# A seven-product group in which block 12 is only ever added by transfers

## The chip, the cores and the metric

The kernel runs on one core of a Trainium2 chip. The metric is the device time of one execution in microseconds (us): 1966.47 is the median of three runs (1966.36 to 1967.82).

## The reference

A decoder layer on 256 tokens (two blocks of 128) with 2048 channels: a SwiGLU FFN of 5632 columns, a mixer of two attention branches, and a second FFN, each with a residual and a layer norm. Nearly all the work is matrix products in float32:

```python
def _swiglu(x, w_gate, w_up, w_down):
    return (jax.nn.silu(x @ w_gate) * (x @ w_up)) @ w_down
...
    c_q, c_kv, k_r, dq, dk, dv, gate_mla, gate_diff = _split_columns(h @ w_in)
...
    y = jax.nn.sigmoid(gate_mla) * (o_mla @ w_br_mla) + jax.nn.sigmoid(gate_diff) * (o_diff @ w_br_diff)
    return y @ w_out
```

## The kernel before, in words

**Split products.** A float32 product is made of three faster ones. Each weight block (128 x 1024, two contraction tiles of 128 by 512 columns) is loaded, cast by ScalarE to a high part (line 154), and VectorE subtracts that from the block to get the low part (line 155). TensorE then does high x high, high x low and low x high (lines 208 to 210). The two parts of a block lie in one of six pairs of a ring (`wring`); a split can start when the products of the unit six before it have read that pair.

**Units and their order.** A unit is a load, a split (`prep`) and its products (`now`). The program issues a unit's load three units ahead of its split, and the split up to four units ahead of its products. Nothing else orders the work: the engines run what was issued, in the order in which a scheduler has put each engine's line, and wait for each other by semaphores. SyncE issues the plain loads, GpSimd (POOL) the transfers that add to what is there, the rows of the hidden layer that go to memory and come back (`hT`), and the mixer's turned rows (`turn`, `turned`) and gates.

**Groups of seven products.** The class `Hybrid` takes two column chunks of 512 (`w0`, `w1`) as a group. Over the first eight of sixteen contraction tiles it multiplies 2 x 2 blocks by seven products instead of eight. The blocks are named by contraction half and chunk: 11 (w0, first), 12 (w1, first), 21 (w0, second), 22 (w1, second). A product has two units (s = 0, 1); in a *wide* group it has a third, half as large (`eraw`), from one contraction tile pair more. The rest of the contraction is *plain* units, p for w0 and q for w1, twelve matmuls each against six in a product's unit. A string gives the order, as "15pp6p72q4q3q" for a wide group.

The weights of the products are sums, made in place on the raw blocks:

- 1 reads 11; 5 reads 11 + 12; 6 reads 11 + 12 + 22; 4 reads 11 + 12 + 22 + 21: VectorE adds to 11 ahead of each of the three (line 430).
- 7 reads 12 + 22: in the FFNs a transfer adds 22 from memory to 12 (line 432); in the mixer (`small`) VectorE does.
- 2 reads 21, and 3 reads 22.

The products' results go to banks X, Z, Y and W, and some of these sums are copied out midway (lines 387, 388), since the next product goes on adding in the same bank.

Each FFN's up projection has ten groups, of which the eight in the middle are wide. The mixer has six narrow ones: three for gates, then dq, dk and dv; in these last three, block 21 uses the buffer of 12 (`share`). A group runs to its end before the next begins. The down projections have a class of their own and aren't part of the change.

## Time and profile before

| | |
|---|---|
| runs, median of 3 | 1966.47 us |
| the profiled execution: its own time, first to last instruction | 1963.9 us, mean granted clock 0.998 |
| TensorE busy | 1952.0 us, 99% |
| VectorE busy | 1779.9 us, 91% |
| ScalarE busy | 1251.5 us, 64% |
| POOL busy | 312.1 us, 16% |
| transfers | 488.86 MB, of which 86.09 MB by GpSimd's queue (q0) |
| adding transfers (line 432) | 40 of 512 KB, 16 of 256 KB |

In the rows below, L154 is line 154 of the kernel; a group of instructions shows its busy time, the mean of one in ns, then the engine's idle time before it and what ended that. PE is TensorE, DVE VectorE, ACT ScalarE, POOL GpSimd, SP SyncE. The view by stretches gives, for each stretch, every engine's busy time and number of instructions, then the granted clock, the mean busy share of the sixteen DMA engines and GB/s. Matmuls are pipelined, so the time from start to start says what one costs.

The first FFN's groups lie at about 40 to 425 us, its down projection follows to about 700, the mixer's groups are at about 720 to 965, and the second FFN's groups at about 1300 to 1690.

### The profile page before, as it was taken

To read this page: it belongs to the slowest core of one execution; us is meant where nothing else is said; L and a number is where in the kernel's file an instruction comes from. 1 tells how busy PE (TensorE), PEld (TensorE's weight loads), DVE (VectorE), ACT (ScalarE), POOL (GpSimd) and SP (SyncE) were. 2 spreads that over 40 slices of the span, in tenths; PEclk is the share of its full clock that TensorE was granted. 3 is DMA by queue.
4 is the path that set the end of the run, shared out by engine and by line. 5 is a ranking of instruction groups with operands and counts; after the bars stand their busy time and mean duration, and the time that the engine had idled before them with its cause. 6 is when DMAs were issued, how large, how long until landed. Compare 5 with 4: busy or idle time off the path is not lost.

```text
span 1963.9 us, 25802 instructions
## 1 busy us (share of the span) xinstructions
PE 1952.0 (99%) x8763; PEld 1617.7 (82%) x8763; DVE 1779.9 (91%) x2189; ACT 1251.5 (64%) x1640; POOL 312.1 (16%) x536
## 2 busy tenths in 40 slices
PE   9999999999999999999999999999999999999998
PEld 7888888888888898888788888888888888888886
DVE  7999999999998879988987777789999999999997
ACT  6666766676655566666667655556676666665662
POOL 0112111122100010102241530001211112210000
PEclk9999999999999999999999999999999999999999
DMA  8978888878776667767685798587888878787773
GB/s 314 289 225 262 270 260 249 257 233 300 272 235 222 210 216 258 239 223 252 211 254 195 237 305 271 201 264 254 252 269 263 250 240 277 241 318 236 277 232 124
DMA packets 150228, 488.86 MB, mean 249 GB/s; under 512 B 21792, under 2 KB 22096, under 8 KB 150096
## 3 DMA queue, kind: packets, MB, share of 16 engines
q1 hardware_dynamic: 119232, 401.00, 59.7%
q0 software_dynamic: 30720, 86.09, 16.8%
q8 instruction: 68, 1.11, 0.2%
q14 instruction: 64, 0.52, 0.1%
q10 hardware_dynamic: 144, 0.13, 0.0%
HBM read 456.73 MB, written 30.41 MB: 248 GB/s over the span
## 4 chain that ended last, share of the span: by engine, by line
PE 95%; DVE 2%; DMA 1%; issue 1%; ACT 0%; POOL 0%; SPq 0%; DVEq 0%; ACTq 0%; POOLq 0%
PE mm L208 30%; PE mm L210 30%; PE mm L209 30%; DVE wring L155 1%; PE tr L208 1%; PE tr L210 1%; PE tr L209 1%; PE tr L673 0%; DMA turned<-turn 0%; ACT wring L154 0%; DMA sraw<-in_wdk_dram 0%; DVE sraw L430 0%; PE tr L1376 0%; PE tr L1304 0%; PE tr L1378 0%
## 5 line engine op out<-in xcount | busy, mean ns | idle before, releaser
L154 ACT CAST wring<-raw 128x1024 fp32r<-128x1024 f32 (+2 forms) x468 | 482.7, 1035 | 323.5 <-PE mm L210 237.6
L155 DVE TENSOR_TENSOR wring<-raw,wring 128x1024 fp32r<-128x1024 f32 (+2 forms) x468 | 557.0, 1198 | 95.6 <-ACT wring L154 93.5
L154 ACT CAST wring<-sraw 128x1024 fp32r<-128x1024 f32 x436 | 453.1, 1052 | 201.7 <-DVE sraw L430 83.6
L155 DVE TENSOR_TENSOR wring<-sraw,wring 128x1024 fp32r<-128x1024 f32 x436 | 520.3, 1218 | 20.6 <-ACT wring L154 17.8
L208 PE MATMUL mm<-wring,h 128*128 128x512 f32 (+2 forms) x1248 | 480.9, 385 | 0.1
L210 PE MATMUL mm<-wring,h 128*128 128x512 f32 (+2 forms) x1248 | 480.3, 385 | 0.0
L209 PE MATMUL mm<-wring,h 128*128 128x512 f32 (+2 forms) x1248 | 479.9, 385 | 0.0
L208 PE MATMUL mm<-wring,xs 128*128 128x512 f32 x776 | 302.2, 389 | 0.5 <-ACT snap L387 0.5
L209 PE MATMUL mm<-wring,xs 128*128 128x512 f32 x776 | 302.1, 389 | 0.0
L210 PE MATMUL mm<-wring,xs 128*128 128x512 f32 x776 | 301.9, 389 | 0.0
L210 PEld LDWEIGHTS mm<-wring,h 128*128 128x128 f32 x1248 | 234.4, 188 | 47.0 <-DVE h L155 0.7
L208 PEld LDWEIGHTS mm<-wring,h 128*128 128x128 f32 x1248 | 234.4, 188 | 46.7 <-ACT h L154 0.6
L209 PEld LDWEIGHTS mm<-wring,h 128*128 128x128 f32 x1248 | 234.4, 188 | 46.1
L430 DVE TENSOR_TENSOR sraw<-sraw,sraw 128x1024 f32<-128x1024 f32 x168 | 199.1, 1217 | 2.0 <-DMA sraw<-in_wdk_dram 1.6
L208 PEld LDWEIGHTS mm<-wring,xs 128*128 128x128 f32 x776 | 145.6, 188 | 31.0 <-ACT snap L387 0.9
L209 PEld LDWEIGHTS mm<-wring,xs 128*128 128x128 f32 x776 | 145.7, 188 | 30.5 <-DVE wring L155 0.3
L210 PEld LDWEIGHTS mm<-wring,xs 128*128 128x128 f32 x776 | 145.7, 188 | 30.2
L719 POOL DMA_DIRECT2D hT<-blocks x176 | 96.8, 563 | 368.3 <-DVE blocks L717 367.2
L209 PE MATMUL mm<-wring,x 128*128 128x512 f32 x336 | 130.9, 390 | 0.2 <-DVE wring L155 0.2
L208 PE MATMUL mm<-wring,x 128*128 128x512 f32 x336 | 130.1, 390 | 0.8 <-ACT wring L154 0.8
L210 PE MATMUL mm<-wring,x 128*128 128x512 f32 x336 | 130.7, 389 | 0.0
L432 POOL DMA_DIRECT2D sraw<-in_gu_dram x40 | 35.6, 892 | 371.4 <-DVE sraw L430 334.5
(328 smaller groups left out, 2292.4 us busy)
## 6 DMA issues: line engine op xcount, KB each, us to landing
sraw<-in_gu_dram SPq DMA_DIRECT2D x160, 512.0 KB, 5.2
raw<-in_gu_dram SPq DMA_DIRECT2D x158, 512.0 KB, 5.0
raw<-in_dn_dram SPq DMA_DIRECT2D x140, 512.0 KB, 4.7
sraw<-in_gu_dram POOLq DMA_DIRECT2D x40, 512.0 KB, 7.5
sraw<-in_dn_dram SPq DMA_DIRECT2D x36, 512.0 KB, 5.4
eraw<-in_gu_dram SPq DMA_DIRECT2D x64, 256.0 KB, 5.8
raw<-in_w_out_dram SPq DMA_DIRECT2D x32, 512.0 KB, 4.3
hraw<-hT POOLq DMA_DIRECT2D x56, 256.0 KB, 5.9
```

The lines of the kernel that those rows point to most:

```text
L154: cast[0] = S.copy(hi, src)
L155: lows[0] = V.tensor_tensor(out=lo, in0=src, in1=hi.bitcast(F32), op=ALU.subtract)
L208: PE.matmul(o, xh, wh, start=first, stop=False, skip_group_check=again)
L209: PE.matmul(o, xh, wl, start=False, stop=False, skip_group_check=again)
L210: PE.matmul(o, xl, wh, start=False, stop=last, skip_group_check=again)
L430: last = V.tensor_tensor(out=R[src][i], in0=R[src][i], in1=R[add[1]][i], op=ALU.add)
L432: nc.gpsimd.dma_start(R["12"][s], source("22", s), accum_op=ALU.add)
L719: nc.gpsimd.dma_start(to.rearrange("(g r) (i f) -> i r g f", g=4, i=4)[i], t[32 * i:32 * (i + 1), :].rearrange("r (g f) -> r g f", g=4))
```

## The change

Block 12 has no buffer any more. After 1 is split, a transfer adds 12 to 11 for product 5; after 6 is split, another adds 12 to 22 for product 7. VectorE adds 22 to 11 for 6, and for 4 adds 11 to 21 as soon as 2 has been split (before, 21 to 11 ahead of 4). The mixer's groups do the same as the FFN's, so `share` goes. Product 3 stands ahead of 6. The first product of a group is issued ahead of the last product (4) and plain units of the group before it (the n in the string); for this the groups are handed over as a list (`run`). Bank Z comes from the three banks of the transposes.

```diff
-            plan = {1: ("11", "11", None, "X"), 5: ("12", "11", ("11", "12"), "Z"), 6: ("22", "11", ("11", "22"), "X"),
-                    7: (None, "12", ("12", "22"), "X"), 2: ("21", "21", None, "Y"), 4: (None, "11", ("11", "21"), "W"),
-                    3: (None, "22", None, "Z")}
+            plan = {1: ("11", "11", None, "X"), 5: (None, "11", None, "Z"), 3: ("22", "22", None, "Z"),
+                    6: (None, "11", "22", "X"), 7: (None, "22", None, "X"), 2: ("21", "21", None, "Y"),
+                    4: (None, "21", None, "W")}
+            added = {1: "11", 6: "22"}
...
-                    banks[n] = mm_bank()
+                    banks[n] = tr_bank() if n == "Z" else mm_bank()
...
-                    if not small and p == 6:
-                        nc.gpsimd.dma_start(R["12"][s], source("22", s), accum_op=ALU.add)
                     pair = [v[:, :tiles * 512] for v in next_pair()]
                     with tc.issue_after(last.ins) if last is not None and not small else nullcontext():
                         split_in_line(not small, *pair, t)
+                    if p in added:
+                        nc.gpsimd.dma_start(R[added[p]][s], source("12", s), accum_op=ALU.add)
+                    elif p == 2:
+                        with nullcontext() if small else behind_split(1):
+                            V.tensor_tensor(out=t, in0=t, in1=R["11"][s], op=ALU.add)
...
-            if self.shared:
-                order = "15pp6p7p3q2q4qq" if seeded else "1p5p6p7p3q2q4qq"
-            elif wide:
-                order = "15pp6p72q4q3q"
-            elif seeded:
-                order = "15pp6p7p2q4q3qq"
-            else:
-                order = "1p5p6p7p2q4q3qq"
+            order = "1p5p36p27qn4qq" if wide else "1p5p36pp27qn4qqq" if self.begun else "1ppp5p3627qn4qqq"
...
+        def run(self, groups):
+
+            parts = [self.group(*g[:-1]) for g in groups]
+            for i, (order, emit) in enumerate(parts):
+                if groups[i][-1] is not None:
+                    groups[i][-1]()
+                for c in order if i == 0 else order[1:]:
+                    if c != "n":
+                        emit(c)
+                    elif i + 1 < len(parts):
+                        parts[i + 1][1]("1")
```

In the second FFN the three blocks that are fetched ahead are now 11, 22 and 21 (before: 11, 12 and 22).

What this does to the lines of the engines is shown at three places.

VectorE, a wide group of the first FFN, from the additions for 6 to the end of 2. Before, `sraw_463`, `464` and `eraw_471` are block 11, `465`, `466` 12, `467`, `468` 22 and `469`, `470`, `eraw_472` 21 (`eraw` holds two blocks each):

```order
L430 TENSOR_TENSOR sraw_463<-sraw_463,sraw_467 128x1024
L430 TENSOR_TENSOR sraw_464<-sraw_464,sraw_468 128x1024
L430 TENSOR_TENSOR eraw_471<-eraw_471,eraw_472 128x512
L155 TENSOR_TENSOR wring_121<-sraw_463,wring_120 128x1024
L155 TENSOR_TENSOR wring_119<-sraw_464,wring_118 128x1024
L155 TENSOR_TENSOR wring_117<-eraw_471,wring_116 128x512
L155 TENSOR_TENSOR wring_115<-raw_1453,wring_114 128x1024
L155 TENSOR_TENSOR wring_105<-sraw_465,wring_104 128x1024
L155 TENSOR_TENSOR wring_103<-sraw_466,wring_102 128x1024
```

After, `sraw_463`, `464` are 11, `465`, `466` 22 and `467`, `468` 21 (`eraw_469` holds 11 and 22, `eraw_470` 21):

```order
L155 TENSOR_TENSOR wring_117<-eraw_469,wring_116 128x512
L438 TENSOR_TENSOR sraw_463<-sraw_463,sraw_465 128x1024
L438 TENSOR_TENSOR sraw_464<-sraw_464,sraw_466 128x1024
L438 TENSOR_TENSOR eraw_469<-eraw_469 128x512
L155 TENSOR_TENSOR wring_115<-sraw_463,wring_114 128x1024
L155 TENSOR_TENSOR wring_105<-sraw_464,wring_104 128x1024
L155 TENSOR_TENSOR wring_103<-eraw_469,wring_102 128x512
L155 TENSOR_TENSOR wring_121<-raw_1469,wring_120 128x1024
L155 TENSOR_TENSOR wring_119<-sraw_467,wring_118 128x1024
L155 TENSOR_TENSOR wring_117<-sraw_468,wring_116 128x1024
L446 TENSOR_TENSOR sraw_467<-sraw_467,sraw_463 128x1024
L446 TENSOR_TENSOR sraw_468<-sraw_468,sraw_464 128x1024
```

Before, 7's split (from `465`) comes one plain unit after 6's. After, the additions for 6 stand directly behind the last split of 3, 2 comes after 6 and a plain unit, and the additions to 21, the last readers of 11, stand behind 2's second split.

VectorE at the change from one group to the next, in the changed kernel:

```order
L155 TENSOR_TENSOR wring_105<-sraw_465,wring_104 128x1024
L155 TENSOR_TENSOR wring_103<-sraw_466,wring_102 128x1024
L155 TENSOR_TENSOR wring_121<-eraw_469,wring_120 128x512
L155 TENSOR_TENSOR wring_119<-raw_1552,wring_118 128x1024
L932 TENSOR_TENSOR hb_1594<-mm_1359,sg_1592 128x256
L155 TENSOR_TENSOR wring_117<-sraw_463,wring_116 128x1024
L155 TENSOR_TENSOR wring_115<-sraw_464,wring_114 128x1024
L155 TENSOR_TENSOR wring_105<-eraw_469,wring_104 128x512
L155 TENSOR_TENSOR wring_103<-sraw_467,wring_102 128x1024
```

That is 7, one plain unit, and then the next group's 1 (from block 11, which was loaded anew) ahead of this group's 4 (from 21). Before, the last use of 11 was 4's split, and a plain unit, 3 and another plain unit stood between it and the next 1.

GpSimd's line in the same stretch, before and after:

```order
L432 DMA sraw_465<-in_gu_dram 128x1024
L432 DMA sraw_466<-in_gu_dram 128x1024
L432 DMA eraw_471<-in_gu_dram 128x512
L719 DMA hT_122<-blocks_1222 32x4x128 x4
L719 DMA hT_122<-blocks_1228 32x4x128 x4
```

```order
L443 DMA sraw_463<-in_gu_dram 128x1024
L443 DMA sraw_464<-in_gu_dram 128x1024
L443 DMA eraw_469<-in_gu_dram 128x512
L443 DMA sraw_465<-in_gu_dram 128x1024
L443 DMA sraw_466<-in_gu_dram 128x1024
L443 DMA eraw_469<-in_gu_dram 128x512
L730 DMA hT_122<-blocks_1236 32x4x128 x4
L730 DMA hT_122<-blocks_1242 32x4x128 x4
```

Three adding transfers a group become six: three to 11, three to 22.

77 lines of the change are left out of this document (42 added, 35 removed).

## The prediction

> **What bounds the kernel now.** I read the page's head first, then the stages, then what TensorE waits for, and last the queues that feed it.
>
> ```profile
> span 1963.9 us, 25802 instructions
> PE 1952.0 (99%) x8763; PEld 1617.7 (82%) x8763; DVE 1779.9 (91%) x2189; ACT 1251.5 (64%) x1640; POOL 312.1 (16%) x536
> ```
>
> TensorE is busy for 99% of the span. Busy is not yet bound, so the next view gives its pace by stretches of 50 us (after the times: PE, PEld, DVE, ACT, POOL, clock, DMA share, GB/s).
>
> ```profile
> 50.00:100.00 50.00, 50.00 (x223) 41.38 (x222) 46.04 (x50) 31.51 (x39) 7.79 (x12) 1.00 0.93 288
> 200.00:250.00 50.00, 50.00 (x222) 41.40 (x221) 49.83 (x56) 32.62 (x42) 7.03 (x11) 1.00 0.86 268
> 600.00:650.00 50.00, 50.00 (x222) 41.42 (x221) 41.86 (x41) 29.83 (x32) 0.00 (x0) 1.00 0.57 183
> 900.00:950.00 50.00, 49.91 (x220) 40.77 (x219) 46.64 (x45) 32.72 (x39) 14.27 (x27) 1.00 0.76 249
> 950.00:1000.00 50.00, 49.49 (x222) 40.63 (x221) 43.56 (x58) 34.48 (x48) 13.85 (x26) 1.00 0.69 221
> 1950.00:2000.00 50.00, 4.94 (x18) 3.03 (x16) 9.37 (x20) 1.25 (x5) 0.00 (x0) 0.91 0.11 42
> ```
>
> 222 matmuls in 50 us are 0.225 us each. That pace is the same with VectorE full (49.83, up projection) and with it at 41.86 and the DMA at 0.57 (down projection). So in the up projection VectorE is close behind TensorE but doesn't hold it up. The tail (1950 on) is not touched. What is left to win is in the mixer's groups, at 900 to 1000; the waits of TensorE, and the rows of the two gaps, say how much.
>
> ```profile
> PE mm L208 <- ACT wring L154: 0.8, 1, 0.8
> PE mm L208 <- ACT snap L387: 0.5, 1, 0.5
> PE mm L209 <- DVE wring L155: 0.2, 1, 0.2
> ...
> 947.65 0.39 PE L210 MATMUL mm<-wring,h 128*128 128x512 f32 x1
> 948.13 0.50 PE L208 MATMUL mm<-wring,h 128*128 128x512 f32 x1
> 948.46 0.39 PE L209 MATMUL mm<-wring,h 128*128 128x512 f32 x1
> ...
> 957.56 0.39 PE L210 MATMUL mm<-wring,h 128*128 128x512 f32 x1
> 958.45 0.50 PE L208 MATMUL mm<-wring,xs 128*128 128x512 f32 x1 [0.51 <-ACT snap L387]
> 958.79 0.39 PE L209 MATMUL mm<-wring,xs 128*128 128x512 f32 x1
> ```
>
> From start to start, against 0.225: 0.48 and 0.33 at 948 lose 0.36 us, 0.89 and 0.34 at 958 lose 0.78. Together 1.1 us of 1963.9: **the whole prize** on the path.
>
> **The change part by part.** The sum is made against the profiled execution, whose own time is its span of 1963.9; the runs' median, 1966.5, lies 2.6 above it (what is outside the span), and I carry that over.
>
> *Removed additions.* Of a wide group's three block additions on VectorE two stay. Rows of 200 to 400, five groups:
>
> ```profile
> L430 DVE TENSOR_TENSOR sraw<-sraw,sraw 128x1024 f32<-128x1024 f32 x30 | 35.3, 1221 | 0.0
> L155 DVE TENSOR_TENSOR wring<-raw,wring 128x1024 fp32r<-128x1024 f32 x30 | 36.2, 1221 | 0.8 <-ACT wring L154 0.8
> L154 ACT CAST wring<-raw 128x1024 fp32r<-128x1024 f32 x30 | 31.6, 1052 | 15.7 <-PE mm L210 15.7
> L154 ACT CAST wring<-eraw 128x512 fp32r<-128x512 f32 x35 | 21.6, 616 | 1.2 <-PE mm L210 1.2
> L430 DVE TENSOR_TENSOR eraw<-eraw,eraw 128x512 f32<-128x512 f32 x10 | 6.9, 687 | 0.0
> ```
>
> One block is 2 x 1.22 + 0.69 = 3.1 us, over 16 wide groups 50 us; the narrow groups (4 in the FFNs, 6 in the mixer that go from four additions to two) save 4 x 2.4 + 6 x 4.9 = 39 us more. All of it is beside TensorE: gain on the path 0.
>
> *Transfers that add.* Per group one plain load of block 12 and one adding transfer (in the mixer none) become two adding ones. Bytes are equal in the FFNs, but an adding byte costs more. From 200 to 360, four groups:
>
> ```profile
> q1 hardware_dynamic: 10325, 33.41, 60.8%
> q0 software_dynamic: 2752, 7.34, 22.7%
> ...
> sraw<-in_gu_dram POOLq DMA_DIRECT2D x8, 512.0 KB, 7.0
> hT<-blocks POOLq DMA_DIRECT2D x32, 64.0 KB, 3.9
> eraw<-in_gu_dram POOLq DMA_DIRECT2D x4, 256.0 KB, 5.3
> ```
>
> Plain: 0.608 x 160 us / 33.41 MB = 2.9 us a MB. q0: 36.3 us, less hT's 2.1 MB at 2.9 (6.1), leaves 30.2 for 5.24 MB: 5.8 a MB. The second adding transfer of 1.31 MB in place of a plain load adds 3.8 us to each 40 us group: the DMA share goes from 0.84 to about 0.93. Throughput still fits; what counts is how late single transfers come. The pages of the two lines give it (min, median, max, 200 to 400; the third is the adding line over the whole span):
>
> ```profile
> DMA to landing us min/median/max: 4.0/5.4/7.5
> ...
> DMA to landing us min/median/max: 5.0/7.0/9.1
> ...
> DMA to landing us min/median/max: 5.0/7.1/11.8
> ```
>
> *Which waits these meet.* A split needs one of six ring pairs, that is the product six units back. This is the commonest wait now, and it gives the lead of the splits over the products:
>
> ```profile
> ACT wring L154 <- PE mm L210: 297.5, 292, 6.3
> ```
>
> A product unit is 6 x 0.225 = 1.35 us, the half one 0.68, a plain unit 2.70; cast and subtraction take 1.05 + 1.22 = 2.27.
> (a) Adding to 11 after product 1, for 5: by the new order the rest of 1, all of 4, two plain units of the old group and one of the new lie between, over 14 us; in a first group 10.8 (1 and three plain units), and the lead of some 5 us comes on top. Nothing to pay.
> (b) Adding to 22, for 7, wide. Time from the end of 3's last split: the three additions follow at once, the first transfer starts at 1.2. By the ring that split ended 6.1 us before its product (the rest of 5, a plain unit and two units of 3 are ahead of it, 7.4, less 1.3 for a half split); 7 starts 0.68 + 3.38 + 2.70 + 3.38 later, at 16.2. It must land within 16.2 - 2.3 - 1.2 = 12.7 us. Largest seen in wide groups: 9.1. In a first group, where 6, 2 and 7 stand together, the same sum gives 10.4, against the 11.8 of the rush at a phase's start: up to 1.4 us in each of three. I take 0.1 each, since the rush at 50 to 100 us (0.93, above) cost TensorE nothing.
> (c) The next group's plain load of 11 now waits for the addition behind 2's split, with only 7 and one plain unit before product 1. Split, second split, addition end 2.4 us after the first split; 2 starts 4.5 after it (3's half unit, 6 and a plain unit, 6.75, less 2.27), 1 at 4.5 + 3.38 + 3.38 + 2.70 = 13.9. It must land within 13.9 - 2.3 - 2.4 = **9.2 us**. Before, it waited for 4's split, ahead of 4, q, 3 and q, and the same sum gives 14. Median 5.4, largest 7.5: still covered, cost 0, but this is the cover that has become thin.
>
> [...]
>
> *The moved products.* 3 ahead of 6 puts 6 us and more between 6 and 7, where one plain unit (2.7) stood and where the 958 gap arose:
>
> ```profile
> 956.88 1.04 ACT wring L154
> 957.92 0.48 ACT snap L387
> ```
>
> ACT copied product 6's bank late, behind casts. The copy of 5's bank now has the 2.7 us cover instead. Gain between 0 and 0.78 at 958; I take 0.7. At 948 ACT stood waiting for a returned transfer whose place doesn't change: 0 to 0.36, I take 0.1.
>
> *Banks, queue of POOL.* Product bank Z moves to the transposes' three banks, of which the groups need at most two: 0. In the mixer the adding transfers share POOL's line with the turned rows, one of which is four stores:
>
> ```profile
> L719 POOL DMA_DIRECT2D turn<-blocks x104 | 56.7, 552 | 165.9 <-DVE blocks L717 143.8 <-DVE ms L1203 18.5 <-issue 2.3
> ```
>
> In the worst place (the last group, eight stores ahead of the second transfer for 7) that is 4.4 us, and the two plain units between 6 and 2 give 5.4: 0, at worst 1 to 2.
>
> **Sum:** -0.8 + 0.3 = -0.5: span 1963.4, with 2.6 outside it 1966.0 us.
>
> **The rivals.**
> *R1, slower: the load of 11 lands late.* One mechanism, at each of 16 wide groups' ends, from 9.2 us on. For it: adding transfers of 22 are in flight just before, and one of 512 KB takes 5.8 x 0.52 = 3.0 us of all engines. Behind one: 5.4 + 3.0 = 8.4, free; behind two: 11.4, 2.2 us a group, 35 in all: 2001 us. With the DMA full, 30 to 60 us shows what landings come to:
>
> ```profile
> q1 hardware_dynamic: 2453, 8.92, 80.9%
> q0 software_dynamic: 274, 1.02, 17.0%
> ...
> sraw<-in_gu_dram SPq DMA_DIRECT2D x8, 512.0 KB, 9.6
> ```
>
> At 9.6 it is 0.4 us a group, 6.4 in all: 1972. Against it: the largest in wide groups is 7.5, and VectorE's spare 3 us let the lead fill again. [...]
> *R2, faster: VectorE was the bound.* 49.83 of 50 would then give back 3.1 us in each of 16 groups: 1916. Against it: 222 matmuls in every stretch, full or not.
> *R3: small new stalls* in first groups (3 x 1.4) and the mixer (2), nothing won: 1972 at most, about 1969 likely.
> *R4: the whole prize,* 1.1, and no cost: 1965.4. That the order doesn't move is excluded by the instruction order.
>
> **How the numbers follow.** What can be told from no change is about 0.2%, 3.9 us. Forecast with R4: 0.67 (own range 1964.3 to 1969); R3 0.11, of which 0.03 over the bound; R1 0.18; R2 0.04. So faster 0.04, same 0.75, slower 0.21. The range 1964.0 to 1974.0 takes the forecast, R3 and the lower half of R1 (to 1974), and leaves out R2 and the rest of R1, 0.04 + 0.09.
>
> **What would show it.** Right: 222 matmuls per 50 us from 200 to 400 with VectorE near 46 of 50, a DMA share near 0.93, q0's bytes up by some 38 MB (a block more in each of 20 FFN groups, 25; two in each of 6 mixer groups, 13), the wait on product 6's copy gone. Wrong: TensorE waiting on line 155 or 154 at product 1 with a DMA ahead of it (R1), a pace above 222 (R2), or new gaps at 60 to 80, 1320 to 1340 or 730 to 960 us (R3).

## The result

The changed kernel takes 2026.08 us (median of four runs, 2024.96 to 2030.44) against 1966.51 for the kernel before, run beside it: a ratio of 1.0308, 95% interval 1.0292 to 1.0323. It is 3% slower, where no change was predicted. The profiled execution has a span of 2023.2 us, against 1963.9.

The head of its page, to be held against the one of before:

```profile
span 2023.2 us, 25924 instructions
PE 1970.7 (97%) x8763; PEld 1619.2 (80%) x8763; DVE 1708.5 (84%) x2109; ACT 1249.0 (62%) x1640; POOL 382.4 (19%) x616
```

The matmuls are as many as before, 8763. VectorE is busy for 71 us less (the prediction had 89, from the lengths of single additions); POOL for 70 us more, in transfers. The same stretches of 50 us as before (PE, PEld, DVE, ACT, POOL, granted clock, DMA share, GB/s):

```profile
50.00:100.00 50.00, 46.81 (x198) 37.70 (x197) 38.00 (x38) 27.51 (x34) 8.76 (x13) 0.97 0.86 270
200.00:250.00 50.00, 47.74 (x209) 38.58 (x208) 45.58 (x54) 32.97 (x43) 14.06 (x22) 1.00 0.88 256
600.00:650.00 50.00, 50.00 (x223) 41.42 (x222) 44.96 (x63) 32.24 (x36) 2.13 (x4) 1.00 0.77 254
900.00:950.00 50.00, 48.65 (x214) 39.63 (x213) 38.34 (x37) 26.98 (x31) 14.58 (x24) 1.00 0.73 219
950.00:1000.00 50.00, 39.68 (x156) 30.90 (x155) 34.07 (x36) 27.97 (x35) 16.76 (x28) 0.90 0.84 249
```

The down projection (600 to 650) keeps its pace, with 223 matmuls. The groups of the networks and of the mixer fall to 209, 198 and 156: every stage that the change touches now has gaps, and VectorE is less busy in them, not more. What TensorE waits for (us in all, times, the longest):

```profile
PE mm L209 <- DVE wring L155: 14.6, 17, 1.1
PE mm L208 <- ACT snap L396: 14.2, 10, 3.0
PE tr L208 <- ACT snap L396: 8.6, 5, 5.2
```

Two names carry it: VectorE's half of a split that comes late, and ScalarE's copy of a bank (line 396, the copies after 5 and 7). One step further back, in ScalarE's waits, stands something else:

```profile
ACT wring L154 <- PE mm L210: 230.3, 210, 8.0
ACT wring L154 <- DMA sraw<-in_gu_dram: 110.2, 71, 4.7
ACT wring L154 <- DMA eraw<-in_gu_dram: 29.9, 38, 1.6
```

Before, the row of `sraw` was 6.6 us in 5 waits. ScalarE now stands 140 us before transfers into the raw blocks. Some of that is only lead given up; the rest is passed on to TensorE.

For the bookkeeping, each matmul's time from start to start above 0.2265 us (28 matmuls from 16.09 to 22.43 us, in the kernel before) is summed by stage: TensorE's *loss*. The kernel before loses nothing in the networks' groups and 2.5 us in the mixer. The changed one loses 19.4 us in the first network, 25.4 in the mixer and 15.3 in the second network. 60.1 less 2.5 are 57.6 of the 59.3 us between the two spans, so these three stages are all but 2 us of it. In the networks 16.8 us of the loss are gaps of up to 1.3 us inside a product (17 of them; most come once in a wide group, inside product 7, and wait for VectorE) and 9.7 us are seven gaps between a matmul into a transposes' bank and the first one into bank X, at unit q, which wait for ScalarE's copy.

**One wide group, followed back.** POOL's line, then ScalarE's, VectorE's and TensorE's (start, duration, what, idle time before it and what ended that), in the changed kernel from 204 us on:

```profile
209.65 1.80 POOL L443 DMA_DIRECT2D sraw<-in_gu_dram  x2 [2.51 <-ACT snap L396]
211.11 1.20 POOL L443 DMA_DIRECT2D eraw<-in_gu_dram  x1
```

```profile
204.53 1.05 ACT L154 CAST wring<-sraw 128x1024 fp32r<-128x1024 f32 x1 [2.01 <-DMA sraw<-in_gu_dram]
...
217.58 1.05 ACT L154 CAST wring<-sraw 128x1024 fp32r<-128x1024 f32 x1 [1.34 <-DVE wring L155]
221.38 1.05 ACT L154 CAST wring<-sraw 128x1024 fp32r<-128x1024 f32 x1 [2.74 <-DMA sraw<-in_gu_dram]
223.77 0.62 ACT L154 CAST wring<-eraw 128x512 fp32r<-128x512 f32 x1 [1.35 <-DVE wring L155]
```

```profile
207.86 2.35 DVE L155 TENSOR_TENSOR wring<-sraw,wring 128x1024 fp32r<-128x1024 f32 x2
...
222.46 1.23 DVE L155 TENSOR_TENSOR wring<-sraw,wring 128x1024 fp32r<-128x1024 f32 x1 [1.97 <-ACT wring L154]
```

```profile
225.77 0.39 PE L208 MATMUL tr<-wring,xs 128*128 128x512 f32 x1
...
246.65 0.50 PE L209 MATMUL mm<-wring,xs 128*128 128x512 f32 x1 [1.13 <-DVE wring L155]
```

The cast at 204.53 is the first half of product 1's split from block 11; VectorE's half of it begins at 207.86 and ends at about 209.1. Then the first adding transfer to 11 can go, at 209.65. Product 5's splits are the casts at 217.58, 221.38 and 223.77: less than 8 us from the first transfer's issue to the first of them. The landings of these three transfers, from that line's page for 208 to 212 us (min, median, max):

```profile
DMA to landing us min/median/max: 7.8/10.8/12.6
```

The second transfer lands at about 221.3 and ends ScalarE's wait of 2.74 us; VectorE idles behind ScalarE. The other two casts also start 0.1 us behind a landing, though their rows name VectorE, and POOL's row names a copy of ScalarE that ended together with VectorE's half.

TensorE does not wait for product 5. Its first matmul (225.77) starts without a gap, 5.9 us behind the end of its first split, and its other two units start 3.4 and 2.7 us behind theirs. The wait was paid out of the splits' lead. From 225.1 to 249 VectorE then works without a gap, through the splits of 3, the additions for 6, the splits of 6 and 2 and the additions behind 2, and comes 1.13 us late with product 7's split, 25 us after the wait. It had no time to spare in which to make up the lead.

### The profile page after: what moved, and what is told of

It is laid out like the page before. It is cut to its first block, busy times and chain, and to the rows that moved or that the text cites. A ratio compares the mean times of both kernels' runs of the same rounds, so it can differ in the third digit from the quotient of the medians.

```text
span 2023.2 us, 25924 instructions
## 1 busy us (share of the span) xinstructions
PE 1970.7 (97%) x8763; PEld 1619.2 (80%) x8763; DVE 1708.5 (84%) x2109; ACT 1249.0 (62%) x1640; POOL 382.4 (19%) x616
## 5 line engine op out<-in xcount | busy, mean ns | idle before, releaser
L154 ACT CAST wring<-sraw 128x1024 fp32r<-128x1024 f32 x436 | 453.9, 1051 | 287.2 <-DMA sraw<-in_gu_dram 110.2
L208 PE MATMUL mm<-wring,h 128*128 128x512 f32 (+2 forms) x1136 | 439.6, 387 | 9.1 <-ACT snap L396 9.0
L210 PE MATMUL mm<-wring,h 128*128 128x512 f32 (+2 forms) x1136 | 438.0, 386 | 0.0
L209 PE MATMUL mm<-wring,h 128*128 128x512 f32 (+2 forms) x1136 | 437.7, 385 | 0.1
L208 PEld LDWEIGHTS mm<-wring,h 128*128 128x128 f32 x1136 | 213.8, 188 | 55.0 <-ACT snap L396 13.5
L210 PEld LDWEIGHTS mm<-wring,h 128*128 128x128 f32 x1136 | 213.8, 188 | 42.3 <-DVE h L155 0.7
L209 PEld LDWEIGHTS mm<-wring,h 128*128 128x128 f32 x1136 | 213.9, 188 | 41.9 <-DVE wring L155 0.7
L209 PE MATMUL mm<-wring,xs 128*128 128x512 f32 x568 | 224.6, 395 | 14.7 <-DVE wring L155 14.6
L208 PE MATMUL mm<-wring,xs 128*128 128x512 f32 x568 | 222.7, 392 | 1.3 <-ACT wring L154 1.0
L210 PE MATMUL mm<-wring,xs 128*128 128x512 f32 x568 | 222.0, 391 | 0.0
L443 POOL DMA_DIRECT2D sraw<-in_gu_dram x80 | 69.9, 896 | 538.2 <-DVE sraw L438 374.5
L209 PEld LDWEIGHTS mm<-wring,xs 128*128 128x128 f32 x568 | 107.2, 189 | 45.0 <-DVE wring L155 23.5
L208 PEld LDWEIGHTS mm<-wring,xs 128*128 128x128 f32 x568 | 107.1, 189 | 24.9 <-ACT wring L154 1.5
L210 PEld LDWEIGHTS mm<-wring,xs 128*128 128x128 f32 x568 | 107.2, 189 | 21.7
L208 PE MATMUL tr<-wring,xs 128*128 128x512 f32 x280 | 110.7, 395 | 8.7 <-ACT snap L396 8.6
L209 PE MATMUL tr<-wring,xs 128*128 128x512 f32 x280 | 110.1, 393 | 1.2 <-DVE wring L155 1.2
L208 PE MATMUL mm<-wring,x 128*128 128x512 f32 x272 | 105.6, 391 | 5.2 <-ACT snap L396 5.2
L210 PE MATMUL tr<-wring,xs 128*128 128x512 f32 x280 | 109.8, 392 | 0.0
```

The lines of the kernel that those rows point to most:

```text
L154: cast[0] = S.copy(hi, src)
L208: PE.matmul(o, xh, wh, start=first, stop=False, skip_group_check=again)
L209: PE.matmul(o, xh, wl, start=False, stop=False, skip_group_check=again)
L210: PE.matmul(o, xl, wh, start=False, stop=last, skip_group_check=again)
L443: nc.gpsimd.dma_start(R[added[p]][s], source("12", s), accum_op=ALU.add)
```

## The experiments

Where no interval is given, a time is from one run, beside a run of the kernel before at 1964.9 to 1966.9 us. The changed kernel's own four runs lie 5.5 us apart, so a difference of that size between two single runs shows nothing by itself. "Lost" is TensorE's loss as defined above: first network / mixer / second network; the changed kernel has 19.4 / 25.4 / 15.3.

### Four parts taken away

**The mixer's adding transfers left out.**

```diff
-                    if p in added:
+                    if p in added and not small:
```

> The changed kernel, with the adding transfers left out of the mixer's four groups alone: blocks 11 and 22 stay as loaded there, so the sums with 12 are missing from the mixer's gates and projections. The feed-forward networks are untouched. Loss of TensorE in the changed kernel, counted against a pace of 0.2265 us a matmul: 19.4 us in the first network's groups, 25.4 us in the mixer (22.6 in gaps, 2.8 at half pace), 15.3 us in the second. Theory A (the mixer loses its time to POOL's line: the adding transfers are issued there, share it with the turn stores and turned rows, and their landings hold the splits): the mixer's loss falls from 25.4 to below 6 us, the time to 2001 to 2007 us, and the networks' losses stay. Rival (the mixer loses its time to the order: no cover for the copy of 7's bank, and ScalarE's line with casts and copies): the four gaps from transposes to the first matmul of unit q stay (6.3 us in all), with most of the rest, and the time stays above 2015.

Measured: 2008.6 us, lost 18.3 / 8.3 / 16.8. The mixer's loss falls by 17 us, and the networks' stays: the stages don't hang together. That is theory A, a little short of its sums (under 6 us, at most 2007). Which property of the transfers does it (their place in POOL's line, their landing, their bytes) isn't told by this run.

**The copy of 7's bank left out.**

```diff
-                     7: lambda: S.copy(n3, banks["X"]), 5: lambda: S.copy(q5, banks["Z"]),
+                     5: lambda: S.copy(q5, banks["Z"]),
...
-                     4: lambda: done(0, 1, banks["W"], n3, ALU.subtract)}
+                     4: lambda: done(0, 1, banks["W"], n2, ALU.subtract)}
```

> The changed kernel, with ScalarE's copy of bank X after product 7 left out; product 4's result takes the copy made after 6 in its place, so that the right half of the lower rows' result is wrong by product 7. Every matmul and every transfer stays. Theory B (q behind 7 has to wait for the copy of 7's bank, whose cover is only 1.35 us): the gaps from unit transposes or from 7's end to the first matmul of q vanish in both networks (9.7 us in seven gaps, and 1.8 us at half pace behind the longest) and in the mixer (6.3 us in four gaps); the time falls by 11 to 18 us, to 2008 to 2015, while the wide groups' gaps inside product 7 (1.3 us each) stay. Rival (q's first matmul waits for its split, or for another reader of the banks): the gaps stay within 3 us in sum, and the time above 2022.

Measured: 2021.1 us, lost 18.0 / 21.4 / 16.7. The gaps to q went, and the time hardly moved: 5 us where 11 to 18 were expected. What TensorE waits for shows where the gain went:

```profile
PE mm L209 <- DVE wring L155: 21.5, 25, 1.2
```

25 waits for VectorE in place of 17, 7 us more. So the copy is not a cause that adds to the other. I read it as one of two places at which the same lateness comes to TensorE.

**The additions behind 2 left out.**

```diff
-                    elif p == 2:
+                    elif p == 2 and small:
```

> The changed kernel, with VectorE's additions of 11 onto 21 behind product 2 left out in the feed-forward networks, so that product 4 multiplies 21 alone there. Theory C (the gaps of 1.3 us inside product 7, once in each wide group, come from VectorE's line: idle while 5's splits wait for transfers, then 16.7 us of work against 12.8 us of products, with the additions behind 2 just ahead of 7's split): 12 or more of the 13 wide gaps vanish, 15 to 17 us less in all, the time 2009 to 2012. Rival (7's split waits for the transfer that adds onto 22, not for VectorE): the gaps stay, the time within 3 us of 2026.

Measured: 2006.5 us, lost 8.1 / 23.6 / 11.1. With 3.1 us less for VectorE in a wide group, its gaps inside 7 are gone (0.8 us left in all on that row). The copy's gaps stay. Theory C had expected a little less gain, 2009 to 2012. This run shows that VectorE's line is too long after the wait, not why it starts late. It also lets the new load of 11 go earlier, and doesn't tell the two apart.

**The transfers onto 11 left out.**

```diff
-                    if p in added:
+                    if p in added and (small or p != 1):
```

> The changed kernel, with the transfers that add 12 onto 11 left out in the feed-forward networks, so that products 5 and 6 multiply 11 and 11 plus 22 there. The additions onto 22 stay. Theory D (the transfers onto 11 land 8 to 13 us after their issue, in a burst with SP's loads, hold 5's splits on ScalarE by some 5 us, and leave VectorE late for the rest of the group): the waits of 5's splits for transfers vanish and with them the 1.3 us gaps inside product 7, 14 to 17 us in all; the first groups' gaps shrink too, by up to 4 us; the time is 2007 to 2012. Rival (VectorE's line is too long by itself between the additions for 6 and 7's split, wherever it starts): the gaps stay at 0.8 us or more each and the time above 2018.

Measured: 1992.9 us, lost 2.5 / 22.8 / 2.5. Both kinds of gap go from the networks' wide groups, more than the expected 14 to 17 us: 30 of 34.7 (the time expected was 2007 to 2012). In a stretch of wide groups TensorE has its pace again, with VectorE as busy as it was forecast for the change:

```profile
200.00:250.00 50.00, 50.00 (x222) 41.42 (x221) 46.88 (x53) 34.97 (x45) 7.86 (x13) 1.00 0.77 240
```

### Why the transfers onto 11 come late

**Plain transfers in place of adding ones,** at the same places and with the same waits; the traces show TensorE, ScalarE and VectorE at the same work in the same order.

```diff
-                        nc.gpsimd.dma_start(R[added[p]][s], source("12", s), accum_op=ALU.add)
+                        if small:
+                            nc.gpsimd.dma_start(R[added[p]][s], source("12", s), accum_op=ALU.add)
+                        else:
+                            nc.gpsimd.dma_start(R[added[p]][s], source("12", s))
```

> The changed kernel, with the transfers onto 11 and 22 in the feed-forward networks overwriting their targets in place of adding to them: the same transfers at the same places, with the same waits, from the same blocks, but plain ones, so the products there multiply 12 where they should multiply sums. Leaving the transfers onto 11 out had taken the networks' loss of TensorE from 34.7 us to 5.0. Theory E (they come late because an addition costs the DMA engines about twice a plain transfer, 5.8 against 2.9 us a MB in the trace before): plain ones land in 6 us or less, the networks lose under 10 us, the time is 1995 to 2003 us. Rival F (they come late because they start only behind the split of product 1 and queue among SP's loads; plain ones would do so too): they land 7 us or more after their issue, the networks lose over 25 us, the time is above 2015.

Measured: 1995.5 us, lost 4.5 / 23.7 / 2.0: theory E, 28 of the networks' 34.7 us. The landings between 100 and 400 us, of the changed kernel's adding transfers first, then of these plain ones:

```profile
DMA to landing us min/median/max: 5.2/7.5/13.1
```

```profile
DMA to landing us min/median/max: 3.4/5.2/8.4
```

The median fell by 2.3 us and the largest by 4.7, and ScalarE's wait for `sraw` in the networks from 110.2 us to 20.1. With no wait in between, this kernel also shows how much time such a transfer has: the cast of 1's first half, the first of 5's casts, and on POOL's line the first transfer to 11. 
```profile
200.98 1.06 ACT L154 CAST wring<-sraw 128x1024 fp32r<-128x1024 f32 x1 [0.30 <-PE mm L210]
...
212.91 2.05 ACT L154 CAST wring<-sraw 128x1024 fp32r<-128x1024 f32 x2
```

```profile
205.66 0.56 POOL L446 DMA_DIRECT2D sraw<-in_gu_dram  x1 [2.56 <-ACT wring L154]
```

11.9 us lie between the casts, and 7.25 from the issue to the second cast: enough for 5.2 and not for 7.5.

The queue's bytes are the same, its share of the DMA engines isn't (packets, MB, share; the changed kernel, then this one):

```profile
q0 software_dynamic: 42240, 123.84, 26.2%
```

```profile
q0 software_dynamic: 40192, 123.84, 19.9%
```

0.262 x 2023.2 less 0.199 x 1993.7 are 133 us, for the 50.3 MB that the networks' transfers move (80 of 512 KB, 32 of 256 KB): 2.65 us a MB for the addition alone. The prediction had 5.8 - 2.9 = 2.9.

**The transfers onto 22 left out,** as many bytes from another place.

```diff
-                    if p in added:
+                    if p in added and (small or p != 6):
```

> The changed kernel, with the transfers that add 12 onto 22 left out in the feed-forward networks, so that product 7 multiplies 11 plus 22 without 12 there. As many bytes go as in the run without the additions onto 11, but from another place. Theory D (the late landings on 11 ahead of 5's splits set the loss): the 1.3 us gaps inside product 7 stay, the networks lose over 25 us of the 34.7, the time is 2014 to 2026. Rival (the DMA engines are full, and any 37 MB less would do): the networks lose under 12 us, as without the additions onto 11 (5.0 us there), and the time is 1993 to 2003.

Measured: 2031.4 us, lost 21.2 / 24.3 / 21.5. Nothing is gained, where the same bytes left out at 11 gave 1992.9 us; relief of the DMA engines as such is not what counts here. The waits for VectorE inside products even rise, from 14.6 us in 17 to 19.3 us in 24. Theory D had 2014 to 2026 us; why the networks lose 8 us more than in the changed kernel stays open.

**Product 5 one unit later.**

```diff
-            order = "1p5p36p27qn4qq" if wide
+            order = "1pp5p3627qn4qq" if wide
```

> The changed kernel with one unit moved in the wide groups of the feed-forward networks: the plain unit p that stood between products 6 and 2 now stands ahead of product 5 (1 p p 5 p 3 6 2 7 q n 4 q q), so that the transfers onto 11 have 2.7 us more, and those onto 22 have 2.7 us less. All is computed. Theory D (5's splits wait for 11's transfers, and VectorE is late from there on): the 1.3 us gaps of the 13 wide groups go or shrink below 0.3 us, 12 to 17 us less, the time is 2009 to 2014. Rival C (VectorE's line from 3 to 7 is too long by itself): with one plain unit less between the additions for 6 and product 7 the gaps stay or grow, and the time is 2024 to 2035.

Measured: 2027.7 us, lost 16.0 / 24.2 / 21.8. The gaps inside 7 went, as theory D has it, and 12 to 17 us of gain did not come; the time is rival C's. One row of TensorE's waits is new, and the place of its longest wait shows what it is (TensorE's rows, then ScalarE's):

```profile
PE mm L208 <- ACT wring L154: 6.6, 13, 1.5
```

```profile
202.63 0.39 PE L208 MATMUL mm<-wring,xs 128*128 128x512 f32 x1
202.85 0.39 PE L208 MATMUL tr<-wring,x 128*128 128x512 f32 x1
204.70 0.50 PE L208 MATMUL mm<-wring,xs 128*128 128x512 f32 x1 [1.46 <-ACT wring L154]
```

```profile
203.60 1.04 ACT L154 CAST wring<-sraw 128x1024 fp32r<-128x1024 f32 x1 [1.52 <-DMA sraw<-in_gu_dram]
```

With the new string the scheduler has also taken the first matmul of q and the first of the next group's product 1 ahead, into product 7, in each wide group; in the changed kernel they stand in their own units. TensorE so waits, inside product 7, for the cast of block 11, and that cast for 11's new load. That is R1's wait, and it comes from an order that the edit brought along. So the run shows that VectorE's gaps go when 5 stands later, and not what the move alone would have gained.

**The next group's product 1 ahead of q.**

```diff
-            order = "1p5p36p27qn4qq" if wide else "1p5p36pp27qn4qqq" if self.begun else "1ppp5p3627qn4qqq"
+            order = "1p5p36p27nq4qq" if wide else "1p5p36pp27nq4qqq" if self.begun else "1ppp5p3627nq4qqq"
```

> The changed kernel with the next group's product 1 moved ahead of the first plain unit q, so that it stands directly behind product 7 (… 2 7 n q 4 q q); all is computed. The copy of 7's bank then has 3.4 us of product 1 as its cover in place of 1.35, and by the ring of six pairs the splits of 1 and 5 stand 1.36 us further apart. Theory D (5's splits wait for adding transfers that have some 7 us from issue to split and land in 7.6, up to 13): the networks lose a little less, 22 to 30 us of the 34.7, the time is 2012 to 2021. Rival B (the cover of 7's copy is a cause of its own): the gaps from transposes to q (9.7 us in the networks, 6.3 in the mixer) go, 13 us or more less, the time is below 2012. Rival R1 of the prediction (the load of 11 lands late): it now has 2.7 us less, about 6.5 us; if it decides, gaps before product 1 appear and the time is above 2030.

Measured: 1997.8 us, lost 6.3 / 21.5 / 5.5. That is rival B's side: the gaps to q are gone from the networks. But it is more than B's 13 us, and the gaps that wait for VectorE shrank as well:

```profile
PE mm L209 <- DVE wring L155: 6.8, 13, 1.1
```

The adding transfers land as late as before (5.3/7.8/13.3 between 100 and 400 us) and ScalarE still waits 99 us for them. So the lateness is the same, and two covers are longer: the copy's by product 1's 3.4 us, which now precede the 1.35 us of q's first half (the expectation put them in its place), and by the ring the way from 1's to 5's split by 1.36. TensorE shows no wait for product 1's block, though its load has 2.7 us less. Leaving the copy out had brought 5 us; it doesn't move the splits, and this edit does. That the second cover makes the difference is my reading of the two runs; no run moved it alone.

### The order without the transfers onto 11

```diff
-                         for n in ("11", "22", "21")}
+                         for n in ("11", "12", "22", "21")}
...
-                for pair in (("11", "22"), ("21",)):
+                for pair in (("11", "22"), ("21", "12")):
...
-            plan = {1: ("11", "11", None, "X"), 5: (None, "11", None, "Z"), 3: ("22", "22", None, "Z"),
+            plan = {1: ("11", "11", None, "X"), 5: ("12", "11", "12", "Z"), 3: ("22", "22", None, "Z"),
...
-            added = {1: "11", 6: "22"}
+            added = {6: "22"}
```

> The new order alone, in networks and mixer: 12 is again loaded plainly into buffers of its own, by SP's queue, and VectorE adds it onto 11 ahead of 5's splits, as before the change; only the adding transfer onto 22 stays. All is computed. VectorE's work is that of the kernel before. Theory D (the transfers onto 11 are the cause, not the order): the networks lose under 8 us and the mixer under 15, the time is 1970 to 1988 us. Rival (the new order costs by itself, since 7 has lost its copy's cover and VectorE, at 49.8 of 50 us in the kernel before, meets its additions in a worse order): the networks lose over 15 us, the time is above 1992.

Measured: 1979.5 us, lost 3.2 / 6.9 / 4.4. VectorE's additions are back, and 46.6 of the 59.6 us are gone. Some 12 us of loss more than in the kernel before are left: the order's, together with the transfers onto 22 and the new place of bank Z, which this run keeps. TensorE's row of copies, of this kernel, names most of it:

```profile
PE mm L208 <- ACT snap L396: 6.6, 5, 2.1
```

Product 1 ahead of q on top of this:

> The new order with 12 loaded plainly and added by VectorE, and with the next group's product 1 ahead of the first q; all is computed. Theory B2 (what the order itself costs is the cover of 7's copy, 1.35 us, where 3.4 us of product 1 now stand): the four gaps from transposes to q in the networks (5.1 us) and the two in the mixer (2.5 us) go; networks under 3 us lost, the mixer 3 to 6, the time 1968 to 1974 us. Rival (VectorE's additions, now 2 and 7 and 1 close together, cost by themselves): the networks lose as much as with q first, 7 us, in other places, and the time stays at 1977 or above.

Measured: 1988.0 us, lost 5.1 / 18.5 / 0.4. In the networks theory B2 holds: the gaps to q are gone, and apart from the first group of the first network (three gaps of 1.2 to 1.5 us from start to start, at 76 to 83 us) next to nothing is left. In the mixer it fell: 18.5 us lost in place of 6.9, in two gaps of 6.6 and 5.2 us, at places where ScalarE copies late:

```profile
PE tr L208 <- ACT snap L396: 11.0, 2, 6.2
```

There the copy's cover isn't the point; ScalarE itself stands still. From 740 to 1030 us it waits 25.9 us for turned rows, against 11.3 us in the run before. So the time is the rival's (1977 or above), for another reason than the rival had.

### The mixer

ScalarE's line of the changed kernel, ahead of TensorE's longest gap:

```profile
980.11 0.62 ACT L750 COPY dkT<-turned 128x512 f32<-128x512 f32 x1 [7.15 <-DMA turned<-turn]
...
990.52 1.27 ACT L154 CAST cn<-turned 128x512 fp32r<-128x512 f32 x2 [5.46 <-DMA turned<-turn]
...
994.10 0.57 ACT L396 COPY snap<-tr 128x512 f32<-128x512 f32 x1
```

Two reads of turned rows that have not landed hold ScalarE for 7.15 and 5.46 us, and the splits and the copy of a bank that stand behind them in its line start only after them (the copy at 994.10); TensorE waits 5.25 us, up to 994.73. (Without the mixer's adding transfers the same two reads wait 2.51 and 4.08 us.) Two runs ask why the turned rows come late.

```diff
-            nc.gpsimd.dma_start(t, to)
+            nc.sync.dma_start(t, to)
...
-                nc.gpsimd.dma_start(back[key], src)
+                nc.sync.dma_start(back[key], src)
```

> The changed kernel with the loads of turned rows (mixer, attention) issued from SP's queue in place of POOL's, so that they no longer stand in one line with the adding transfers; all is computed. Leaving the mixer's adding transfers out had taken the mixer's loss from 25.4 us to 8.3. Theory A1 (that gain was POOL's line: adding transfers wait there for splits and hold up the turned rows, and ScalarE's line stands at their use): the mixer loses 12 us or less, and the time is 2008 to 2014. Rival A2 (it was the transfers' own landings and VectorE's additions): the mixer still loses over 20 us, the time stays at 2020 or above, or rises where SP's loads queue behind a turned row.

```diff
-                        nc.gpsimd.dma_start(R[added[p]][s], source("12", s), accum_op=ALU.add)
+                        if small:
+                            nc.gpsimd.dma_start(R[added[p]][s], source("12", s))
+                        else:
+                            nc.gpsimd.dma_start(R[added[p]][s], source("12", s), accum_op=ALU.add)
```

> The changed kernel, with the mixer's transfers onto 11 and 22 overwriting in place of adding (12 is multiplied there where sums should be); the networks are untouched. The transfers keep their places in POOL's line and their waits. Theory A1 (the mixer loses by POOL's line: transfers that wait for splits hold up the turned rows behind them): the mixer's loss stays at 18 us or more of 25.4, the time is 2018 to 2026. Rival A2 (it loses by the double cost of an addition, as the networks do): the loss falls below 12 us, the time to 2008 to 2014.

Measured: with the turned rows on SP's queue 2017.3 us, lost 19.1 / 10.7 / 18.0; with plain transfers in the mixer 2008.5 us, lost 19.5 / 10.1 / 15.6. Each takes 15 of the mixer's 25.4 us, so neither A1 nor A2 as I had put them is right: A1 had expected the second run to change nothing. (The first gains less in all: attention, whose turned rows moved too, loses 10.0 us, against 5.4 in the changed kernel.)

A turned row goes to memory and back: VectorE's blocks are stored (`turn`), and when the stores have landed the row is loaded (`turned`). POOL's line ahead of the wait of 7.15 us, then the same load with plain transfers, then without transfers:

```profile
962.47 0.88 POOL L443 DMA_DIRECT2D sraw<-in_wdv_dram  x1 [13.63 <-DVE wring L155]
963.60 0.85 POOL L443 DMA_DIRECT2D sraw<-in_wdv_dram  x1 [0.26 <-DVE wring L155]
964.22 2.47 POOL L730 DMA_DIRECT2D turn<-blocks  x4
973.74 0.56 POOL L742 DMA_DIRECT2D turned<-turn  x1 [7.05 <-DMA turn<-blocks]
```

```profile
959.77 0.56 POOL L745 DMA_DIRECT2D turned<-turn  x1 [5.37 <-DMA turn<-blocks]
```

```profile
957.78 0.56 POOL L742 DMA_DIRECT2D turned<-turn  x1 [4.11 <-DMA turn<-blocks]
```

VectorE ended the blocks at 963.92, so the stores hardly waited in POOL's line. But behind two adding transfers they landed in 7.5 to 8.0 us, behind plain ones in 4.6 to 5.8, with none in 2.6 to 4.0, and the load landed in 6.4, 5.4 and 4.8 us. From the blocks' end to the row's landing that is 16.2, 13.2 and 11.5 us. At the other place of this kind (914 us) it is 16.0, 13.8 and 15.0, so there the transfers cost less.

Eight of the mixer's twelve turned rows are loaded by one line. Their landings from 740 to 1010 us, in order: the changed kernel; plain transfers; no transfers in the mixer; turned rows on SP's queue.

```profile
DMA to landing us min/median/max: 3.0/7.1/9.9
```

```profile
DMA to landing us min/median/max: 3.8/5.5/7.5
```

```profile
DMA to landing us min/median/max: 2.8/4.2/5.2
```

```profile
DMA to landing us min/median/max: 2.8/3.5/6.2
```

The difference sits in four of them, which are issued right behind an adding transfer: 7.9 to 9.9 us, against 5.0 to 7.5 with plain transfers and 3.1 to 5.2 with none. Over all twelve the medians are only 5.8, 5.2, 5.0 and 4.7. So the wait in POOL's line was the wrong half of my theory, and the queue behind it is the right one: stores and loads landed later behind adding transfers (7.5 to 8.0 and 6.4 us at the first place, 2.6 to 4.0 and 4.8 without). ScalarE's waits for turned rows come to 27.0, 19.5, 18.9 and 15.5 us in the four kernels, 7 to 12 us less where TensorE loses 15 to 17 less. What else the three edits gain isn't separated. Some 7 us of the mixer's loss lie at 769 to 875 us, before the first of these rows is loaded (925 us). With plain transfers 2 us of them stay, with the turned rows on SP's queue 5; I take it that there the adding transfers act on the splits themselves, as in the networks.

### The repairs together

The plain 12 and the turned rows on SP's queue:

> Both repairs together: the new order with 12 loaded plainly and added onto 11 by VectorE, and the turned rows' loads on SP's queue; all is computed. If the transfers onto 11 and POOL's line are the two causes, and act apart, the losses are those of the two runs each in its stage: networks under 8 us, mixer 10 or less, the time 1966 to 1980 us, no faster than the kernel before, whose products stand at TensorE's pace. If a third cause is left (the order), the time stays above 1990.

Measured: 1978.7 us, lost 3.9 / 2.8 / 4.1. Each stage does as expected, and attention now loses 9.1 us where the kernel before loses 4.7.

All three edits:

> The new order with 12 loaded plainly, product 1 ahead of q, and turned rows loaded by SP's queue; all is computed. If adding onto 11, the copy's cover and the turned rows on POOL's queue are all there is, the networks lose under 3 us and the mixer under 3, the time is 1966 to 1971 us: no faster than the kernel before by more than 1 us, since that runs at TensorE's pace in these stages. A time below 1964 would need something that the pace of 0.2265 us a matmul hides; above 1974 a third cause is left.

Measured: 1976.5 us, ratio to the kernel before 1.005, 95% interval 1.0033 to 1.0067, from three rounds; lost 3.8 / 4.3 / 0.4. That is 5 us above what was expected. The loss in attention is 10.0 us, and a row that in the changed kernel was one wait of 0.5 us has grown (TensorE's turn of a tile that VectorE makes):

```profile
PE tr L1176 <- DVE p L1330: 4.3, 3, 2.8
```

So the third edit has a price in the stage behind the mixer, which I had not counted: 5.3 us of loss more than before. With the first network's 3.8 us and the mixer's 1.8 above before, that is the 10 us. Ahead of the longest of the three waits (2.75 us, at 1043.60) ScalarE again stands before a turned row, for 2.35 us at 1033.88, with the exponentials behind it that VectorE's tile is made from; from 1000 to 1070 us it waits for no plain load. The edit has also put 129 of TensorE's matmuls from 1021 to 1077 us in another order, so it isn't shown that the price is the queue's.

The adding transfers kept, the other two edits made:

> The changed kernel with its adding transfers kept, product 1 ahead of q, and turned rows loaded by SP's queue; all is computed. With product 1 ahead of q alone the networks lost 11.8 us and the mixer 21.5. Theory (the two repairs act apart, and what is left is the late landing on 11): networks 10 to 13 us lost, the mixer 8 to 11, the time 1984 to 1990. Rival (with the covers back the adding costs nothing, as it was predicted): the time is below 1975.

Measured: 1991.8 us, lost 6.8 / 10.3 / 6.6. Theory, with the time 2 us over its range by attention's 9.2 us. With both covers back the networks still lose 13.4 us, 9.2 more than with 12 loaded plainly. None of the versions beats the kernel before, and in the stages of the change none could by more than some 2.5 us, since its loss there is that small.

## Why the prediction was wrong, point by point

- **What bounds the kernel** was right: TensorE's pace, also in the slow version wherever no gap stands (the run without the transfers onto 11 has 222 matmuls in 50 us again). So was that the removed additions are worth nothing on the path: the kernel before keeps this pace with them, and with them back and the transfers onto 11 gone, the new order takes 47 us less than the changed kernel.
- **Bytes and their price** were right: q0 grew by 37.75 MB (38 predicted), and the addition costs 2.65 us a MB beyond a plain transfer (2.9 predicted). VectorE stands at 45.6 of 50 (46 predicted), the DMA share at 0.88 rather than 0.93, in stretches that the gaps make longer.
- **Wait (a) is the step that failed**: "over 14 us ... and the lead of some 5 us comes on top. Nothing to pay." (14.9 from the start of product 1; "the rest of 1" and what follows give 13.5.) It put the landing against the start of product 5 and so spent the lead as if it were free. For the lead to stay, the transfer has to land before 5's *split*, which is ahead of its product by the same lead as 1's split, so the lead cancels. By the ring's rule, which the prediction itself used for (b) and (c), the splits of 1 and 5 are nine units apart, and their products' time is taken six units earlier: 0.68 + 3.4 + 2.7 + 3.4 + 1.36 = 11.5 us. The trace of the plain transfers has 11.9. Of these, 4.7 pass before the transfer can go, because VectorE's half of 1's split comes that much behind ScalarE's (in the changed kernel 5.1). 7.3 us were left, against landings of 7.5 in the median and up to 13.1. That sum, done before the run, would have shown a time that is just about used up by the 7.0 of the prediction's own rows. What the prediction put at nothing was the spending of the lead: TensorE did not wait at 5, but VectorE could not make the lead up again and came late at 7, in 13 of the 16 wide groups.
- **The landing time** was taken as one transfer's (7.0, with 11.8 as the exception of a phase's start). The three transfers to 11 go out within 2 us, between loads by SP: 7.8, 10.8 and 12.6. What this burst cost was set by its last landing, 12.6 us (the cast at 223.77), not by its median.
- **Wait (b)** for 22 held: with these transfers left out the loss doesn't fall. **Wait (c)** and with it R1 did not decide either. ScalarE does wait for 11's new load (2.0 us at 204.53), but TensorE doesn't, and with 2.7 us less for that load the kernel got faster.
- **The moved products**: the gain at 958 us and the thinner cover of 5's bank were thought of (no run shows that gain by itself); that 7's copy now stands directly ahead of q, with 1.35 us for it, was missed, though the order string shows it. In the order alone it costs 5.1 us in the networks and 2.5 in the mixer.
- **POOL's line in the mixer** was costed by the issue times ("4.4 us, and the two plain units ... give 5.4: 0, at worst 1 to 2"). The price was not the issue but the landing of what stands behind adding transfers, the turned rows' stores and loads, with ScalarE held at their reads (7.15 and 5.46 us). Plain transfers, or SP's queue for the loads, each give back 15 of 25 us, part of it by the splits.
- **The rivals**: R3 named first groups and mixer, with 4.2 and 2 us; the mixer alone lost 23 us more than before, and most of the networks' loss sits in the wide groups, which R3 left out. R1 (but for the run with 5 one unit later), R2 and R4 did not happen. The true rival was R1's mechanism one block over, on the transfer that adds to 11 rather than on its plain load. Of POOL's transfers of 12, whole and half blocks, the fastest plain one landed in 3.4 us (the run with plain transfers), and no adding one in under 5.0. An addition's price on the DMA engines was nearly double a plain transfer's (2.65 us a MB on top of 2.9).

Not settled: how much of the networks' loss belongs to the late landing and how much to the thin covers. Each, taken away alone, gives back most of it (30 us by leaving the transfers out, 23 by moving product 1), so they are not terms of a sum. The first group's gap in the first network (3.4 us at 82) was not tested by itself.

## What to carry to other kernels

The time that a transfer has runs from the moment its target is free (the second reader's end, not the first's) to the next *split* or cast that reads it; a lead that stands ahead of both ends cancels. A wait beyond that time need not stop TensorE where it arises; it uses up lead, and comes back as a gap where the engine that should make it up has no time to spare (here ScalarE's 2.74 us before the cast at 221.38, and TensorE's 1.13 us before 246.65). Take for it the last landing of the whole burst, from rows with the DMA engines as full as they will be, and give each queue that shares the line the same look. ScalarE carried its waits of 7.15 and 5.46 us on to the splits and the copy behind them, and TensorE stood for 5.25 us: ask what else the waiting engine has to copy or cast before the time is up.

## What the runs showed of the hardware

**Behind three of its gaps TensorE ran at half pace,** 0.43 us from start to start in place of 0.23. TensorE's rows of the changed kernel around 994 us (start, duration):

```profile
994.73 0.80 PE L208 MATMUL tr<-wring,xs 128*128 128x512 f32 x1 [5.25 <-ACT snap L396]
995.32 0.63 PE L209 MATMUL tr<-wring,xs 128*128 128x512 f32 x1
...
998.62 0.40 PE L208 MATMUL tr<-wring,xs 128*128 128x512 f32 x1
```

From start to start a matmul takes 0.43 us up to 998.3, then 0.23 again; the granted clock is 0.50 from 994.7 to 998.4 us and 0.99 behind that. This gap of 5.6 us so cost 1.8 us more than itself. Around 82 us the half pace comes later:

```profile
82.25 0.51 PE L208 MATMUL mm<-wring,x 128*128 128x512 f32 x1 [3.05 <-ACT snap L396]
...
83.80 0.63 PE L208 MATMUL mm<-wring,xs 128*128 128x512 f32 x1
```

The half pace begins at 83.8 us, six matmuls after work went on, and lasts 3.4 us (clock 0.51). Here the idle time was 3.05 us. At 965.2 us half pace follows an idle time of only 2.10 us, at the end of 9 us of which TensorE was busy for 4.2. So idle times of 2.10 and 3.05 us had half pace behind them here; the single gaps of 1.3 us in the wide groups have none (0.23 us from start to start behind the one at 246.65).

**Plain transfers right behind an adding one on POOL's queue landed later than without it.** The turned rows' loads right behind one landed in 7.9 to 9.9 us, and in 3.1 to 5.2 us without it; four stores behind two of them in 7.5 to 8.0 us, and in 2.6 to 4.0 without. SP's plain loads into the raw blocks (`sraw<-in_gu_dram`, median, whole span) went only from 5.2 us in the kernel before to 6.1 in the changed one.
